# A decoder trunk's MLP: chunks with on-chip operands, against two phases with DRAM operands and a one-level Strassen product

## The chip, the core and the metric

The kernel runs on one core of a Trainium2 chip as a single launch. The metric is the device time of that launch in microseconds (us), lower is better. The profile is one further execution of the same program, taken by the hardware profiler. TensorE does the matmuls (PE in the profile, PEld for its weight loads), VectorE is DVE, ScalarE is ACT, GpSimd is POOL, and SyncE (SP) issues most of the DMAs.

## The reference, cut to what matters

A trunk of two layers on 1024 tokens of width 1024. Each layer has an attention mixer (compressed, selected and window attention in layer 0, sliding-window attention with sinks in layer 1) and an MLP, with norms and gates around both. The change is in the MLP:

```python
def squared_relu_mlp(h, w_up, w_down):      # h (1024, 1024), w_up (1024, 4096), w_down (4096, 1024)
    a = jax.nn.relu(h @ w_up)
    return (a * a) @ w_down

for i in range(DEPTH):                      # DEPTH = 2
    ...
    h = modulate(rms_norm(x, norm_g[i, 2]), sh2, sc2)
    y = squared_relu_mlp(h, mlp_w_up[i], mlp_w_down[i])
    x = x + (1 + g2)[:, None, :] * rms_norm(y, norm_g[i, 3])
```

All values are float32.

## The kernel before

Every large product is made of float32 operands split exactly into a high and a low float32r part. `mm3` (lines 558 to 563) adds hi*hi, hi*lo and lo*hi into one PSUM bank, so one product of a 128-row contraction tile costs three matmuls of 128x128 by 128x512, each with its own weight load. `weight` (line 539) loads a 512 KB piece of a weight matrix into one of three `raw` buffers, ACT copies it to the high part `wh` (line 554), and DVE subtracts to get the low part `wl` (line 555). Both parts take one 4 KB-per-partition buffer each from the pool of 37 slots, from which nearly all large tiles come. Small tiles of 2 KB per partition come from the tag `t2` with 8 buffers. PSUM has eight banks, handed out in turn by `bank`.

The MLP walks over the 4096 hidden features in tiles of 128, in chunks of two tiles (14 chunks, then one of four; `CHUNKS`). In a chunk, `up` computes the hidden tile for both halves of the tokens (eight contraction tiles, 24 matmuls for each half). ACT takes relu out of PSUM and squares it into the high part `ah`, DVE squares it again (line 1226) and subtracts to get the low part `al` (line 1227). Then `down` multiplies: for each of eight token tiles t and two column halves h, the chunk's two hidden tiles (6 matmuls) are summed in a PSUM bank, and `evac` adds the bank to the running sum `y[t]` in SBUF (line 1242; chunk 0 copies on ACT instead). Left operands never leave SBUF. The next chunk's weights are loaded among these steps.

The program is emitted as a list of main steps of about 1.3 us of TensorE each (`go`), with other steps spread among them (`spread`), or queued to run some steps later (`later`, `chain`). The scheduler of the tile framework then fixes an order for each engine, and buffers are handed out as they come free. In layer 0 the 56 `side` steps, each a 512 KB load of `ada_w` (into the same three `raw` buffers) and a DVE multiply-add (line 315), are spread over all chunks of the MLP.

When the last chunk has finished token tile t, `post` runs: it loads the residual `x`, squares and sums y on ACT (line 502), multiplies by the gate row (line 503; on POOL for the first seven tiles of layer 1, otherwise on DVE), takes the root on POOL (line 440), adds into x on DVE (line 511) and stores x. In layer 0 `finish_tile` then norms the tile (line 461), and after each fourth tile turns four of them into h^T, with a split on DVE (lines 487 and 488). Layer 1's first projection follows at once. In layer 1 the launch ends there.

Of the kernel before, what the change touches and what calls it, by code (L numbers as in the profile page):

```python
# [9 lines left out]
F32 = mybir.dt.float32  # L10
# [19 lines left out]
NCH = [2] * 14 + [4]  # L30
CHUNKS = [range(sum(NCH[:c]), sum(NCH[:c + 1])) for c in range(len(NCH))]
# [47 lines left out]
def spread(a, b):  # L79
    """The steps of b with those of a evenly among them, each before a step of b."""  # L80
    out, n = [], 0
    for k, f in enumerate(b):
        while n < len(a) and n * len(b) <= k * len(a):
            out.append(a[n])
            n += 1
        out.append(f)
    return out + a[n:]


class Trunk:  # L90
    """Products in float32: every operand is split exactly into hi + lo (both float32r), and
    hi*hi + hi*lo + lo*hi accumulate in PSUM."""
# [228 lines left out]
    def ada_cols(self, l, m, acc, dst):  # L321
        """dst [128, 8]: the chunk's values, feature k*128+p at [p, k]."""
# [18 lines left out]
    def ada_first(self):  # L341
        """As ada_pre for the first norm, by halves of the features: half(h) gives the loads and the steps."""
# [52 lines left out]
    def ada_pre(self, l, which, raw=None):  # L395
        """Steps of A = g (1 + scale) and B = shift as columns, for the norm before mixer (0) or MLP (1)."""
# [13 lines left out]
    def ada_gate(self, l, which):  # L410
        """Steps of (1 + gate) g of the norm after mixer (0) or MLP (1), a row in DRAM."""
# [37 lines left out]
    def norm_stages(self, x, out, t):  # L449
        """out[t] = x / rms(x)"""  # L450
# [41 lines left out]
    def gated(self, y, x, gate, eng=None):  # L492
        """(steps for the halves of y, stages after them) of x += gate * y / rms(y); y(h): [128, 512]."""
# [21 lines left out]
    def finish_tile(self, t, x, xr, col, hT):  # L515
        """Norms a finished token tile; after the fourth of a half also turns them into h^T."""
# [41 lines left out]
    def mm3(self, out, s, m, first, last):  # L558
        """out += s.T @ m with s, m = (hi, lo)."""
# [5 lines left out]
    def weights(self, w, rows, c0, n, eng=None, turned=False):  # L565
        """(steps, list): the steps fill the list with (hi, lo) [128, n] for each of the row tiles of w."""
# [8 lines left out]
    def product(self, out, terms, evac):  # L575
        """Main steps: out() = the sum of s.T @ m over terms (functions that give s, m), then evac."""
# [67 lines left out]
    def rope(self, t, src, dst, nh):  # L644
        """dst (SBUF [128, nh*64]) = rotated src (PSUM)."""
# [28 lines left out]
    def vstack(self, src, dst):  # L674
        """dst [128, n, 128] = (hi | lo) of src [128, n * 64] in PSUM."""
# [5 lines left out]
    def nsa_project(self, hT, w):  # L681
        """Chunks (loads, main steps) of the projections and of the compression."""
# [4 lines left out]
        # kc, vc: X[z][r // 6][64 * (r % 2):][:, r % 6 // 2, i, head] is hi (z = 0) or lo (1) of token 16 i + r;  # L687
        # at i = 64 + y it is pe[16 y + r]
# [102 lines left out]
    def compress(self, X, m):  # L791
        """(loads, main steps) of the compressed keys (m = 0) or values (1)."""
# [61 lines left out]
    def q_load(self, i, j, two):  # L854
        """[128 (hi, lo: d), 4 heads, 128 tokens]; loaded together with that of the next block (two = 0) or group (1)"""
# [17 lines left out]
    def masked(self, out, s, mask, nm, init):  # L873
        """out = -(s + mask) / 8 and nm = its minimum (the maximum's negative)."""
# [45 lines left out]
    def o_out(self, o, o32):  # L920
        """o32 [128, 2, 128] = the two halves of o's partitions added, heads on their partitions."""
# [69 lines left out]
    def kv_load(self, j):  # L991
        """Steps that load the K^T stacks (selected, window) and the V stacks (selected, window) of kv head j."""
# [14 lines left out]
    def nsa_unit(self, i, j):  # L1007
        """Steps of the scores and of the products with V for block i, kv head j."""
# [5 lines left out]
        def scale(ps, l, b):  # L1014
            """scales the four P by gate / l"""
# [104 lines left out]
    def importance(self, pc):  # L1120
        """The blocks' importance [128, 16] from the four heads' probabilities."""
# [10 lines left out]
    def select(self, i, imp):  # L1132
        """The mask (0 or NEG) of the selected blocks and of the causal bound, [128, (i + 1) * 128]."""
# [407 lines left out]
```

## Time and profile before

| | |
|---|---|
| Time, median of 3 runs (lowest to highest) | 2641.11 us (2639.13 to 2643.16) |
| Span of the profiled execution, first to last instruction | 2637.3 us |
| Median of the runs less that span | 3.8 us |
| Mean granted TensorE clock | 0.988 |
| PE busy | 2543.5 us, 96% of the span |
| DVE, ACT, POOL busy | 1691.7, 1098.3 and 648.6 us |
| Moved by DMA | 271.37 MB, 103 GB/s over the span |

A matmul's busy time overlaps that of the next one, so PE's rate is read from the starts of matmuls or from their number in a stretch, not from their durations. A granted clock of 1.00 is the higher of TensorE's two levels, 2.4 GHz.

### The profile page before, as it was taken

The numbers are of one execution on the slowest core, as the hardware profiler recorded it, in microseconds if no ns is written. First come the engines' busy times: TensorE is split into PE (matmuls) and PEld (weight loads), VectorE is DVE, ScalarE is ACT, GpSimd is POOL, SyncE is SP. The second block draws the span as 40 slices with busy tenths as digits, with TensorE's granted clock in tenths as the row PEclk, the third lists the DMA queues.
The fourth block names the chain that finished last, engine by engine and source line by source line (L and its number), as shares of the span: only waits on it lengthen the run. The fifth ranks groups of instructions, "written<-read, shape, count | busy, mean of one in ns | idle before, by whom it ended". The sixth has DMA issues, their size and how long they took to land.

```text
span 2637.3 us, 35655 instructions
## 1 busy us (share of the span) xinstructions
PE 2543.5 (96%) x12742; PEld 2125.0 (81%) x12742; DVE 1691.7 (64%) x3739; ACT 1098.3 (42%) x2451; POOL 648.6 (25%) x904
## 2 busy tenths in 40 slices
PE   6999999999989999999999999889999999999998
PEld 4789888888877788888888888767788888888887
DVE  6875589999975756565656477577744544444445
ACT  3642478898862421212121244477742121212122
POOL 4431666556641000000000004487600000000003
PEclk8999999999999999999999999989999999999999
DMA  7388412212256533233323244353221111111113
GB/s 269 119 286 254 156 65 82 79 50 77 65 125 149 158 96 96 80 112 97 95 80 96 64 147 154 107 153 87 65 72 56 42 57 46 56 40 56 40 49 135
DMA packets 199656, 271.37 MB, mean 103 GB/s; under 512 B 12388, under 2 KB 136504, under 8 KB 199480
## 3 DMA queue, kind: packets, MB, share of 16 engines
q1 hardware_dynamic: 170680, 239.74, 28.9%
q0 software_dynamic: 28800, 29.36, 4.6%
q8 instruction: 100, 1.64, 0.3%
q14 instruction: 76, 0.62, 0.1%
HBM read 213.47 MB, written 55.59 MB: 102 GB/s over the span
## 4 chain that ended last, share of the span: by engine, by line
PE 56%; DVE 5%; POOL 2%; issue 2%; ACT 1%; DMA 1%; POOLq 0%; DVEq 0%; ACTq 0%
PE b L561 18%; PE b L563 18%; PE b L562 18%; DVE p L875 1%; DVE x L511 1%; POOL r L440 1%; DVE wl L555 0%; DMA adaw<-in_ada_w_dram 0%; PE b L871 0%; POOL qv L626 0%; POOL p L1332 0%; DVE yg L503 0%; DVE pT L901 0%; DVE hl L488 0%; PE o L916 0%
## 5 line engine op out<-in xcount | busy, mean ns | idle before, releaser
L561 PE MATMUL b<-hh,wh 128*128 128x512 f32 x1344 | 524.9, 392 | 3.9 <-DVE hh L487 2.0
L562 PE MATMUL b<-hl,wh 128*128 128x512 f32 x1344 | 525.5, 391 | 0.3 <-DVE hl L488 0.2
L563 PE MATMUL b<-hh,wl 128*128 128x512 f32 x1344 | 524.2, 390 | 1.2 <-DVE wl L555 1.2
L1242 DVE TENSOR_TENSOR y<-b,y 128x512 f32<-128x512 f32 x448 | 306.3, 689 | 190.0 <-PE b L563 188.8
L561 PE MATMUL b<-wh,ah 128*128 128x512 f32 x1024 | 399.7, 390 | 0.0
L562 PE MATMUL b<-wl,ah 128*128 128x512 f32 x1024 | 398.4, 389 | 0.0
L563 PE MATMUL b<-wh,al 128*128 128x512 f32 x1024 | 397.5, 389 | 0.0
L554 ACT ACTIVATE wh<-w 128x1024 fp32r<-128x1024 f32 (+1 forms) x183 | 212.2, 1162 | 367.9 <-PE b L562 299.3
L1224 ACT ACTIVATE r<-b 128x512 f32<-128x512 f32 x128 | 76.1, 595 | 628.9 <-PE b L563 628.9
L555 DVE TENSOR_TENSOR wl<-w,wh 128x1024 fp32r<-128x1024 f32 (+1 forms) x171 | 229.1, 1341 | 155.7 <-ACT wh L554 87.2
L561 PEld LDWEIGHTS b<-hh,wh 128*128 128x128 f32 x1344 | 252.9, 188 | 57.5 <-ACT wh L554 2.3
L563 PEld LDWEIGHTS b<-hh,wl 128*128 128x128 f32 x1344 | 253.0, 188 | 54.1 <-DVE wl L555 1.9
L562 PEld LDWEIGHTS b<-hl,wh 128*128 128x128 f32 x1344 | 253.1, 188 | 52.9 <-DVE hl L488 1.6
L879 ACT ACTIVATE p<-p,nm 128x256 f32<-128x256 f32 (+7 forms) x384 | 250.4, 656 | 55.3 <-DVE nm L875 52.6
L440 POOL TENSOR_TENSOR r<-ms,mhalf 128x1 f32<-128x1 f32 x64 | 46.0, 725 | 853.8 <-DVE ms L439 848.5
L1226 DVE TENSOR_TENSOR r<-r 128x512 f32<-128x512 f32 x128 | 88.4, 691 | 247.1 <-ACT ah L1225 246.6
L1019 POOL TENSOR_SCALAR p<-p,rl,gate 128x640 f32<-128x640 f32 (+7 forms) x256 | 199.4, 791 | 134.4 <-DVE rl L1017 83.1
L901 DVE TENSOR_TENSOR pT<-b,pT 128x512 fp32r<-128x512 f32 (+1 forms) x334 | 214.8, 656 | 17.5 <-ACT pT L900 15.8
L563 PEld LDWEIGHTS b<-wh,al 128*128 128x128 f32 x1024 | 192.2, 188 | 39.9
L561 PEld LDWEIGHTS b<-wh,ah 128*128 128x128 f32 x1024 | 192.2, 188 | 39.7
L562 PEld LDWEIGHTS b<-wl,ah 128*128 128x128 f32 x1024 | 192.3, 188 | 39.6
L900 ACT ACTIVATE pT<-b 128x512 fp32r<-128x512 f32 (+1 forms) x334 | 185.6, 578 | 42.6 <-PE b L894 33.9
(241 smaller groups left out, 4294.7 us busy)
## 6 DMA issues: line engine op xcount, KB each, us to landing
adaw<-in_ada_w_dram SPq DMA_DIRECT2D x96, 512.0 KB, 4.2
w<-in_mlp_w_up_dram SPq DMA_DIRECT2D x64, 512.0 KB, 4.2
w<-in_mlp_w_down_dram SPq DMA_DIRECT2D x64, 512.0 KB, 3.6
x<-x SPq DMA_DIRECT2D x48, 512.0 KB, 3.4
w<-in_nsa_w_in_dram SPq DMA_DIRECT2D x18, 512.0 KB, 5.9
x<-in_x_dram SPq DMA_DIRECT2D x16, 512.0 KB, 5.6
kv<-k POOLq DMA_DIRECT2D x16, 512.0 KB, 4.9
qd<-qh SPq DMA_DIRECT2D x32, 256.0 KB, 2.1
```

Of the source, the lines that this page charges most:

```text
L554: nc.scalar.activation(h_, r_, AF.Copy)
L555: (eng or (nc.gpsimd if early else nc.vector)).tensor_tensor(l_, r_, h_.bitcast(F32), op=ALU.subtract)
L561: mm(out, s[0], m[0], start=first, stop=False)
L562: mm(out, s[0], m[1], start=False, stop=False)
L563: mm(out, s[1], m[0], start=False, stop=last)
L879: self.nc.scalar.activation(p, p, AF.Exp, scale=-1.0, bias=nm, accum_out=l)
L900: nc.scalar.activation(x[:, 0, 0:w], pt[:, 0:w], AF.Copy)
L901: nc.vector.tensor_tensor(x[:, 1, 0:w], pt[:, 0:w], x[:, 0, 0:w].bitcast(F32), op=ALU.subtract)
L1019: nc.gpsimd.tensor_scalar(ps[g], ps[g], rl[:, g:g + 1], gate[:, g, b:b + 1], op0=ALU.mult, op1=ALU.mult)
L1224: nc.scalar.activation(r, pt, AF.Relu)
L1226: nc.vector.tensor_tensor(r, r, r, op=ALU.mult)
L1242: nc.vector.tensor_tensor(y[t][:, sl], pt, y[t][:, sl], op=ALU.add)
```

## The change

The MLP becomes two phases. `mlp_up` computes all 32 hidden tiles of the layer one after another. For each it keeps a float32 tile u (relu on ACT, one square on DVE, no split). For every pair q of hidden tiles (a, b) `combine` makes five sums or differences of token halves on POOL, and SP writes seven left operands of 128x512 to a DRAM tile: b1, a0+b1, b0-b1, a0+b0, a1-a0, a0 and a1+b1, where a0 is the first half of the tokens of tile a.

`mlp_down` computes the second product as a one-level Strassen product: contraction halves are the even and the odd hidden tiles, row halves the token halves, column halves those of the output. It makes four passes g over the 16 pairs q. Passes 0 to 2 compute two of the seven products each, pass 3 the seventh. A product has four token tiles, one PSUM bank each, and is summed over the whole contraction in that bank. So passes 0 to 2 hold all eight banks for 16 items (g, q), and pass 3 four. For each item `load` brings the left operands and W_down rows from DRAM (1.25 MB in passes 0 and 2, 1.0 in pass 1, 0.5 in pass 3, in units of 1024 x 1024 bytes); `prep` makes the right operand's sums on POOL (two adds, one, two, none) and splits both operands (high part on ACT, low part on DVE). Loads are emitted three items ahead, the splits one item ahead. At the end of a pass `evac` adds and subtracts the banks into y. Token tiles 0 to 3 are finished by pass 2 and go to `post` during pass 3; tiles 4 to 7 finish one after another in the last four items, which run token tile by token tile.

The 56 side steps of layer 0 are now spread over `mlp_up` alone. Comments and docstrings are removed, which changes no instruction. The core of the diff:

```diff
-NCH = [2] * 14 + [4]
-CHUNKS = [range(sum(NCH[:c]), sum(NCH[:c + 1])) for c in range(len(NCH))]
+UT = HID // P
...
-        def down(Wd, A, t, h, c):
...
+    def mlp(self, hT, w_up, w_down, first, side, post, last):
+        sd = self.mlp_up(hT, w_up, first, side)
+        self.mlp_down(sd, w_down, post, last)
+
+    def mlp_up(self, hT, w_up, first, side):
...
+        def up(u, hf):
+            def evac(pt):
+                if hf == 0:
+                    U[u] = self.slot("u", F32, [P, 2, 512])
+                r = self.t2("r")
+                nc.scalar.activation(r, pt, AF.Relu)
+                nc.vector.tensor_tensor(U[u][:, hf], r, r, op=ALU.mult)
+                if hf == 1 and u % 2 == 1:
+                    self.later(lambda: self.chain(combine(u // 2)), 1)
...
+        def combine(q):
+            a, b = U.pop(2 * q), U.pop(2 * q + 1)
+            d = self.tc.dram_tile([P, 7, 512], F32, name=f"s{self.n}_{q}")
...
+            def put():
+                nc.sync.dma_start(d[:, 0], b[:, 1])
+                nc.sync.dma_start(d[:, 5], a[:, 0])
+                nc.sync.dma_start(d[:, 1:3], z[0])
+
+            def put2():
+                nc.sync.dma_start(d[:, 3:5], z[1])
+                v = self.t2("sy")
+                nc.gpsimd.tensor_tensor(v, a[:, 1], b[:, 1], op=ALU.add)
+                nc.sync.dma_start(d[:, 6], v)
+
+            A, B = ALU.add, ALU.subtract
+            return [two(0, (a[:, 0], b[:, 1], A), (b[:, 0], b[:, 1], B)), put,
+                    two(1, (a[:, 0], b[:, 0], A), (a[:, 1], a[:, 0], B)), put2]
+
+        order = [(0, 0), (1, 0), (0, 1), (1, 1)] + [(u, hf) for u in range(2, UT) for hf in range(2)]
...
+        self.go(spread(side, steps))
...
+    def mlp_down(self, sd, w_down, post, last):
...
+        items = [(g, q) for g in range(4) for q in range(n_q)]
...
+        def load(g, q):
+            m = 1 if g == 3 else 2
+            s, w = (self.slot(x, F32, [P, 2, 512]) for x in ("sr", "wr"))
+            nc.sync.dma_start(s[:, 0:m], sd[q][:, 2 * g:2 * g + m])
...
+                nc.sync.dma_start(w, two(rows[g < 2]))
+                e = None
+                if g != 1:
+                    e = self.t2("we")
+                    nc.sync.dma_start(e, rows[0][:, 0:512] if g == 0 else rows[1][:, 512:1024])
...
+            def sums():
...
+                if g == 0:
+                    t(w[:, 0], w[:, 0], e, op=ALU.subtract)
+                    t(w[:, 1], w[:, 1], e, op=ALU.add)
+                elif g == 1:
+                    t(w[:, 0], w[:, 0], w[:, 1], op=ALU.add)
+                elif g == 2:
+                    t(w[:, 0], w[:, 0], w[:, 1], op=ALU.add)
+                    t(w[:, 1], w[:, 1], e, op=ALU.subtract)
+
+            def split(k):
...
+                nc.scalar.activation(hi, r, AF.Copy)
+                nc.vector.tensor_tensor(lo, r, hi.bitcast(F32), op=ALU.subtract)
+                ready.setdefault((g, q), []).append((hi, lo))
...
+        def evac(g, z, b):
+            o, c = banks.pop((z, b)), b + 4
+            if (g, z) == (0, 0):
+                copy(b, 0, o), copy(c, 0, o)
+            elif (g, z) == (0, 1):
+                add(b, 0, o), copy(c, 1, o)
+            elif (g, z) == (1, 0):
+                add(b, 0, o)
+            elif (g, z) == (1, 1):
+                copy(b, 1, o), add(b, 0, o, ALU.subtract)
+            elif (g, z) == (2, 0):
+                add(c, 1, o)
+            elif (g, z) == (2, 1):
+                add(b, 1, o), add(c, 1, o)
+                self.later(lambda: post(b, y[b]), 12 * b + 4)
+            else:
+                add(c, 0, o), add(c, 1, o, ALU.subtract)
+                self.later(lambda: post(c, y[c]), 0)
+
+        def mms(g, q, z, b):
+            if q == 0:
+                banks[z, b] = self.bank()
+            s, t = (tuple(v[:, z] for v in x) for x in ready[g, q])
+            self.mm3(banks[z, b], tuple(v[:, b * P:b * P + P] for v in s), t, q == 0, q == n_q - 1)
+            if q == n_q - 1:
+                evac(g, z, b)
+
+        TAIL = 4
+        main = [[lambda z=z, b=b, g=g, q=q: (mms(g, q, z, b), mms(g, q, z, b + 1)) for z in range(2 - (g == 3)) for b in (0, 2)]
+                for g, q in items[:-TAIL]]
+        tail = items[-TAIL:]
+        main.append([lambda b=b, k=k: [mms(*tail[j], 0, b) for j in (k, k + 1)] for b in range(4) for k in range(0, TAIL, 2)])
...
+        for n, steps in enumerate(main):
+            extra = [f for k in ahead(n + 1) for f in prep(*items[k])]
+            upto = min(len(items), n + 4 + max(0, n - len(main) + 2 * TAIL))
+            extra = [lambda k=k: load(*items[k]) for k in range(loaded, upto)] + extra
...
+            self.go(spread(extra, steps))
```

## Rows read from the trace of the kernel before

**Rows 1.** The page's line of busy time by engine.

```profile
PE 2543.5 (96%) x12742; PEld 2125.0 (81%) x12742; DVE 1691.7 (64%) x3739; ACT 1098.3 (42%) x2451; POOL 648.6 (25%) x904
```

**Rows 2.** Stretches: length, engines' busy time (instructions), clock, DMA share, GB/s.

```profile
132.00:198.00 66.00, 60.77 (x380) 54.90 (x381) 51.44 (x69) 27.53 (x33) 20.82 (x12) 0.95 0.86 287
881.00:1589.00 708.00, 704.93 (x3183) 581.18 (x3183) 420.31 (x571) 180.65 (x265) 8.08 (x12) 1.00 0.33 102
1740.00:1752.00 12.00, 4.64 (x17) 3.24 (x18) 12.00 (x31) 11.38 (x28) 11.85 (x14) 0.63 0.65 209
1929.00:2630.00 701.00, 700.58 (x3107) 579.93 (x3105) 337.75 (x458) 160.09 (x248) 22.91 (x23) 1.00 0.19 57
2050.00:2500.00 450.00, 450.00 (x1987) 372.59 (x1987) 219.27 (x292) 84.87 (x120) 0.00 (x0) 1.00 0.16 47
```

**Rows 3.** Timeline of PE in layer 1's MLP: start, duration, instruction.

```profile
2100.38 0.39 PE L561 MATMUL b<-wh,ah 128*128 128x512 f32 x1
...
2101.06 0.39 PE L561 MATMUL b<-wh,ah 128*128 128x512 f32 x1
```

**Rows 4.** By line, 2050 to 2500: count, busy us, mean ns, idle.

```profile
L1242 DVE TENSOR_TENSOR y<-b,y 128x512 f32<-128x512 f32 x171 | 118.2, 691 | 91.2 <-PE b L563 90.5
...
L555 DVE TENSOR_TENSOR wl<-w,wh 128x1024 fp32r<-128x1024 f32 x41 | 50.1, 1222 | 42.6 <-PE b L562 42.6
L554 ACT ACTIVATE wh<-w 128x1024 fp32r<-128x1024 f32 x40 | 42.0, 1049 | 0.0
...
L1227 DVE TENSOR_TENSOR al<-r,ah 128x512 fp32r<-128x512 f32 x40 | 27.6, 690 | 1.0
...
L1224 ACT ACTIVATE r<-b 128x512 f32<-128x512 f32 x40 | 24.0, 599 | 349.7 <-PE b L563 349.7
```

**Rows 5.** By line, whole run, same columns.

```profile
L315 DVE SCALAR_TENSOR_TENSOR ada<-adaw,cond,ada 128x1024 f32<-128x1024 f32 x70 | 90.0, 1286 | 65.5 <-DMA adaw<-in_ada_w_dram 65.2
...
L511 DVE SCALAR_TENSOR_TENSOR x<-yg,r,x 128x1024 f32<-128x1024 f32 x32 | 41.6, 1301 | 14.8 <-POOL r L440 14.7
...
L487 DVE CAST hh<-h 128x512 fp32r<-128x512 f32 x64 | 28.1, 467 | 15.4 <-ACT h L485 12.5 <-PE b L871 2.9
...
L461 DVE TENSOR_SCALAR xr<-x,r 128x1024 f32<-128x1024 f32 x32 | 24.6, 780 | 17.8 <-POOL r L440 17.0 <-PE b L562 0.7
...
L503 POOL TENSOR_TENSOR yg<-y,gbc 128x512 f32<-128x512 f32 x14 | 18.0, 1294 | 665.0 <-DVE y L1242 665.0
```

**Rows 6.** Timeline of DVE in layer 0's projections.

```profile
141.28 1.22 DVE L555 TENSOR_TENSOR wl<-w,wh 128x1024 fp32r<-128x1024 f32 x1
142.97 1.77 DVE L555 TENSOR_TENSOR wl<-w,wh 128x1024 fp32r<-128x1024 f32 x1 [0.47 <-ACT wh L554]
145.22 1.75 DVE L555 TENSOR_TENSOR wl<-w,wh 128x1024 fp32r<-128x1024 f32 x1 [0.48 <-ACT wh L554]
```

**Rows 7.** Timeline of POOL in the same stretch.

```profile
143.62 2.27 POOL L626 TENSOR_TENSOR qv<-qv,qr 128x512 f32<-128x512 f32 x1
146.64 1.48 POOL L628 TENSOR_TENSOR qr<-qv,qh 128x512 f32<-128x512 f32 x1 [0.75 <-ACT qh L627]
```

**Rows 8.** DMA issues, whole run: count, KB each, us to landing.

```profile
w<-in_mlp_w_up_dram SPq DMA_DIRECT2D x64, 512.0 KB, 4.2
w<-in_mlp_w_down_dram SPq DMA_DIRECT2D x64, 512.0 KB, 3.6
...
qd<-qr SPq DMA_DIRECT2D x32, 256.0 KB, 2.0
```

**Rows 9.** Waits in layer 0's MLP, 960 to 1500: total us, times, longest.

```profile
ACT wh L554 <- PE b L562: 266.5, 29, 19.3
...
DVE ada L315 <- DMA adaw<-in_ada_w_dram: 37.8, 20, 5.0
```

**Rows 10.** Timeline of DVE at the end of the run.

```profile
2629.71 0.68 DVE L1242 TENSOR_TENSOR y<-b,y 128x512 f32<-128x512 f32 x1
...
2632.26 1.28 DVE L511 SCALAR_TENSOR_TENSOR x<-yg,r,x 128x1024 f32<-128x1024 f32 x1 [0.66 <-POOL r L440]
```

More of the change, by code (lines that the diff above doesn't have):

```diff
@@ L1231, in up @@
             return self.product(self.bank, [lambda k=k: term(k) for k in range(KT)], evac)
-        def down(Wd, A, t, h, c):
-            sl = slice(h * 512, h * 512 + 512)
-            def evac(pt):
-                if c == 0:
-                    if h == 0:
-                        y[t] = self.slot(name="y")
-                    nc.scalar.activation(y[t][:, sl], pt, AF.Copy)
-                else:
-                    nc.vector.tensor_tensor(y[t][:, sl], pt, y[t][:, sl], op=ALU.add)
-                if c == nch - 1 and h == 1:
-                    post(t, y[t])
-            def term(u):
-                return tuple(v[:, t * P:(t + 1) * P] for v in A[u]), tuple(v[:, sl] for v in Wd[u])
-            return self.product(self.bank, [lambda u=u: term(u) for u in range(len(CHUNKS[c]))], evac)
@@ L1250, in mlp, with two, f @@
-        side = list(side)
-        for c in range(nch):
-            (_, W), (dload, Wd) = loads
-            A, ups, downs = [], [], []
-            for hf in range(2):
-                for u in range(len(CHUNKS[c])):
-                    if hf == 0:
-                        ups.append(lambda: A.append((self.slot("ah", F32R), self.slot("al", F32R))))
-                    ups += up(W, A, u, hf)
-            for t in range(NT):
-                for h in range(2):
-                    downs += down(Wd, A, t, h, c)
-            nxt = last
-            if c + 1 < nch:
-                loads = self.mlp_loads(w_up, w_down, c + 1)
-                nxt = loads[0][0]
-            k = -(-len(side) // (nch - c))
-            n = 0 if c + 1 < nch else len(ups) // 2
-            self.go(spread(side[:k], ups[:n] + spread(dload, ups[n:]) + spread(nxt, downs)))
-            side = side[k:]
+        def combine(q):
+            a, b = U.pop(2 * q), U.pop(2 * q + 1)
+            d = self.tc.dram_tile([P, 7, 512], F32, name=f"s{self.n}_{q}")
+            sd.append(d)
+            z = {}
+            def two(n, *ops):
+                def f():
+                    z[n] = self.slot("sx", F32, [P, 2, 512])
+                    for k, (x, y, op) in enumerate(ops):
+                        nc.gpsimd.tensor_tensor(z[n][:, k], x, y, op=op)
+                return f
+            def put():
[10 more added lines that the diff above has]
+                    two(1, (a[:, 0], b[:, 0], A), (a[:, 1], a[:, 0], B)), put2]
@@ new lines, in mlp_up, with prep, new, copy @@
+        order = [(0, 0), (1, 0), (0, 1), (1, 1)] + [(u, hf) for u in range(2, UT) for hf in range(2)]
+        steps = []
+        for n, (u, hf) in enumerate(order):
+            ld = [loads[u + 2 - (n < 4) * u + (n < 4) * (n - 2)]] if (n >= 4 and hf == 0 and u + 2 < UT) or n in (2, 3) else []
+            steps += spread(ld, up(u, hf))
+        self.go(spread(side, steps))
+        return sd
+    def mlp_down(self, sd, w_down, post, last):
+        nc = self.nc
+        n_q = len(sd)
+        items = [(g, q) for g in range(4) for q in range(n_q)]
+        y, raw, ready, banks = [None] * NT, {}, {}, {}
+        def load(g, q):
+            m = 1 if g == 3 else 2
+            s, w = (self.slot(x, F32, [P, 2, 512]) for x in ("sr", "wr"))
+            nc.sync.dma_start(s[:, 0:m], sd[q][:, 2 * g:2 * g + m])
+            rows = [w_down[(2 * q + x) * P:(2 * q + x + 1) * P] for x in range(2)]
+            two = lambda r: r.rearrange("p (h c) -> p h c", h=2)
+            if g == 3:
+                nc.sync.dma_start(w[:, 0], rows[0][:, 0:512])
+                e = None
+            else:
+                nc.sync.dma_start(w, two(rows[g < 2]))
+                e = None
+                if g != 1:
+                    e = self.t2("we")
+                    nc.sync.dma_start(e, rows[0][:, 0:512] if g == 0 else rows[1][:, 512:1024])
+            raw[g, q] = s, w, e
+        def prep(g, q):
+            u = {}
+            def sums():
+                s, w, e = u["r"] = raw.pop((g, q))
+                t = nc.gpsimd.tensor_tensor
+                if g == 0:
[7 more added lines that the diff above has]
+            def split(k):
+                r = u["r"][k]
+                if g == 3:
+                    h = self.slot("st", F32R, [P, 2, 512])
+                    hi, lo, r = h[:, 0:1], h[:, 1:2], r[:, 0:1]
+                else:
+                    hi, lo = (self.slot("st", F32R, [P, 2, 512]) for _ in range(2))
+                nc.scalar.activation(hi, r, AF.Copy)
+                nc.vector.tensor_tensor(lo, r, hi.bitcast(F32), op=ALU.subtract)
+                ready.setdefault((g, q), []).append((hi, lo))
+            return [sums, lambda: split(0), lambda: split(1)]
+        def new(t, h):
+            if y[t] is None:
+                y[t] = self.slot(name="y")
+            return y[t][:, h * 512:h * 512 + 512]
+        def copy(t, h, o, eng=None):
+            if eng:
+                eng.tensor_copy(new(t, h), o)
+            else:
+                nc.scalar.activation(new(t, h), o, AF.Copy)
+        def add(t, h, o, op=ALU.add):
+            v = y[t][:, h * 512:h * 512 + 512]
+            nc.vector.tensor_tensor(v, v, o, op=op) if op == ALU.subtract else nc.vector.tensor_tensor(v, o, v, op=op)
+        def evac(g, z, b):
[13 more added lines that the diff above has]
+                self.later(lambda: post(b, y[b]), 12 * b + 4)
+            else:
+                add(c, 0, o), add(c, 1, o, ALU.subtract)
[12 more added lines that the diff above has]
+        main.append([lambda b=b, k=k: [mms(*tail[j], 0, b) for j in (k, k + 1)] for b in range(4) for k in range(0, TAIL, 2)])
+        ahead = lambda n: [n] if n < len(items) - TAIL else list(range(len(items) - TAIL, len(items))) if n == len(items) - TAIL else []
+        loaded = 3
+        for n in range(loaded):
+            load(*items[n])
+        for f in prep(*items[0]):
+            f()
+        for n, steps in enumerate(main):
+            extra = [f for k in ahead(n + 1) for f in prep(*items[k])]
+            upto = min(len(items), n + 4 + max(0, n - len(main) + 2 * TAIL))
+            extra = [lambda k=k: load(*items[k]) for k in range(loaded, upto)] + extra
+            loaded = upto
+            if len(main) - n <= 8:
+                extra += last[:-(-len(last) // (len(main) - n))]
+                last = last[-(-len(last) // (len(main) - n)):]
+            self.go(spread(extra, steps))
@@ L1456, in run @@
                     else:
-                        steps = spread(first[0][0], steps)
+                        steps = spread(first[0][:2], steps)
                     self.go(steps)
@@ L1478, in run @@
                 out(NT - 1)
-                self.go(spread(first[0][0], extra))
+                self.go(spread(first[0][:2], extra))
             self.mark("mlp")
```

24 lines of the change are left out of this document (6 added, 18 removed).

## The prediction

> **What bounds the kernel now.** Read the busy line first: PE is busy 96% of the span, and DVE, next, 64% [rows 1]. A share over a span hides stages, so the stretches come next. The MLP of layer 1 fills 1929 to 2630, that of layer 0 roughly 881 to 1589; inside layer 1's, from 2050 to 2500, PE is busy for all of 450.0 us at clock 1.00 while DVE works 219.3, ACT 84.9, POOL 0, and DMA engines are at a share of 0.16 [rows 2]. The reader is to see one saturated engine and four with room. PE's rate comes from its starts: one trio takes 2101.06 - 2100.38 = 0.68 us, 0.2267 us a matmul [rows 3], and the count agrees, 450/1987 = 0.2265 [rows 2]. One MLP has 2 x 1536 = 3072 matmuls, 696.4 us at that rate. The stretches of the two layers are 708 and 701 [rows 2], so some 12 and 5 us of the two MLPs are anything else. There is little to win here but matmuls.
>
> **Removed.** For each pair of hidden tiles `down` now makes 8 x 2 x 2 = 32 three-matmul sums; the new phase makes 7 x 4 = 28. That is 12 matmuls less for each of 16 pairs in two layers, 384, at 0.2267: 87.0 us, all on PE. DVE also loses the accumulation (691 ns, 448 times in all) and the low part of the hidden tile (690 ns), ACT one square; they had slack, so this counts for nothing by itself [rows 4].
>
> **The first phase.** PE's 1536 matmuls are unchanged, 348.2 us. For each pair (21.8 us) POOL gets five 128x512 adds of 1.29 [rows 5], 6.5 us, on an engine that is idle here. SP gets five stores of 1.84 MB together (29.4 MB a layer). In layer 0 the 56 loads of `ada_w` (29.4 MB) now fall into this half, beside W_up's 16.8 MB: 75.5 MB in 348 us, 217 GB/s. The nearest row is 132 to 198, 287 GB/s at share 0.86, which is 333 at a full share [rows 2]; so 0.65. A W_up piece holds a `raw` buffer for 4.2 (landing) + 1.05 + 1.22 = 6.5 us [rows 4, 8], an `ada_w` piece for about 4.2 + 1.29 = 5.5 [rows 5]: 32 x 6.5 + 56 x 5.5 = 516 us of holding in 348, half of what three buffers offer (1044). Bounds: nothing, or, if two of the three buffers were lost to waiting in turn, 516 - 348 = 168. DVE did wait for `ada_w` 20 times, 37.8 us, in 540 us of the old kernel, and PE did not feel it [rows 2, 9]. I take 2 us.
>
> **The second phase, in its steady state.** An item of passes 0 to 2 is 24 matmuls, 5.44 us of PE. Against it:
> - ACT: two copies of 1024 at 1.05 = 2.1 us [rows 4].
> - DVE: two subtractions of 1024 at 1.22 = 2.4 us [rows 4].
> - POOL: at most two adds at 1.29 = 2.6 us [rows 5].
> - DMA: 1.31 MB (passes 0 and 2), 241 GB/s; over a layer 64 x 1.05 = 67.1 MB in 1344 x 0.2267 = 304.7 us, 220 GB/s, a share of 0.66 by the same 333.
>
> Each alone has half of the time free, so the loads and splits, emitted one to three items ahead, are hidden by PE. But DVE and POOL are not independent. Where both ran two-input operations, DVE's subtractions ended at 144.74 and 146.97 and took 1.77 and 1.75 instead of 1.22, and POOL's ended at 145.89 and 148.12 after 2.27 and 1.48 [rows 6, 7]. One of each ends every 2.23 us. So an item's two pairs need 4.46 us of the 5.44: covered, with 18% to spare, and I add nothing. The Trainium skill (SBUF — State Buffer, "Who interferes with whom") says that a DVE instruction with two SBUF inputs and a GpSimd instruction that reads SBUF exclude each other for the whole instruction. By that the two pairs would need 2 x (1.22 + 1.29) = 5.02 us, still under 5.44; the rows give 4.46, so they overlap somewhat more than that rule allows.
>
> **Ends of passes.** All eight banks close within one item. After pass 0, twelve ACT copies of 0.60 and four DVE adds of 0.69; after pass 1, four copies and eight adds; after pass 2, twelve adds [rows 4]. A bank is wanted again one item after its last matmul, 4.1 to 5.4 us later, by the first use in the next pass. ACT's 7.2 us run beside the 5.44 us of the closing item and are wanted one by one, so they just fit if no split stands before them. Bounds: none, or all of the longer engine's work in the open, 7.2 + 5.5 + 8.3 = 21 us a layer, 42 in all. The copies are wanted in the order in which they come, so I take 3.
>
> **Other seams.** Between phases, item 0 needs only its loads and splits, ready long before: 1 us a layer; at worst a load, an add pair and a split in the open, 3.6 + 2.6 + 1.05 + 1.22 = 8.5 each [rows 4, 5, 8]. In layer 0's pass 3 (192 matmuls, 43.5 us) DVE has 16 x 2 x 0.69 = 22.1 of splits, 8.3 of closing pass 2, four token tiles' `post` and norm at 2 x 0.69 + 1.30 + 0.78 = 3.5 (13.8), eight h^T splits at 0.47 + 0.69 (9.3) and four weight splits (4.9): 58.4 us [rows 4, 5]. That is 15 over, unless splits were made ahead while pass 2 left DVE idle. Bounds 0 and 15; I take 5. The last four token tiles then need 2.72 us of PE each but 3.5 + 1.4 of DVE, so layer 1 begins with a backlog of 9 us and the 9.3 of h^T behind it; the first projection has 16 x 6 x 0.2267 = 21.8 us of work on the first token half as cover: 3 us, bounds 0 and 10. At the very end two adds instead of one follow the last matmul, and `post` comes every 2.72 us instead of 5.44; the end chain from the add to the last DVE write was 2633.54 - 2629.71 = 3.8 us [rows 10] and grows by 2; bounds 0.7 (the extra add) and 4.6 (that, and one token tile's 2 x 1.29 on POOL and 1.30 on DVE in turn).
>
> **The sum.** -87.0 + 2 + 3 + 2 + 5 + 3 + 2 = -70.0. Against the profiled execution: 2637.3 - 70.0 = 2567.3, and with the 3.8 us around its span 2571.1; the median of the runs shown, 2641.1, stands for the same. I forecast 2571 us, with 2554 (every seam free) to 2588 for this case.
>
> **The rivals.**
> 1. *Passes close in the open.* Speaks for it: eight banks are all that there are, and none is left to rotate into. Against: the next pass wants them in the order of their closing. Time: 42 in place of 3, 2571 + 39 = 2610. The Trainium skill (Perfetto Trace Analysis, "Matmuls" under Optimizing Tensor Performance) asks that groups rotate through banks so that emptying one overlaps the next group; here that overlap exists only across passes. Chance 0.10.
> 2. *DVE and POOL become the bound of passes 0 and 2.* For: rows 6 show DVE idle another 0.47 before each contended subtraction, waiting for ACT. If that stays, an item is 2 x (1.22 + 1.29 + 0.48) = 5.98 us, 0.54 more than PE, in 64 items: +35, 2606. Against: splits of later items are independent, so the wait should be filled. It binds from 5.44 us an item on. Chance 0.08.
> 3. *Layer 0 is crowded:* the first phase's buffers or pass 3's DVE cost their 15 to 25 more: 2586 to 2596. For: ACT stood up to 19.3 us before a buffer that PE had to free [rows 9], so work ahead is limited by the 37 slots. Chance 0.10.
> 4. *The loads don't keep up: slower.* If the stream has one transfer in flight, an item takes 3.6 + 3.6 + 2.0 = 9.2 us in passes 0 and 2, 7.2 in pass 1 and 4.0 in pass 3 [rows 8]: 16 x (18.4 + 7.2 + 4.0) = 474 a layer against 304.7, +338 in all, 2571 + 338 = 2909. It decides below 67.1 MB in the old 348 us, 193 GB/s. And a PE that waits pays more: in 1740 to 1752 it was busy for 4.64 of 12 us and was granted 0.63 of the clock [rows 2]. Against: 287 GB/s in 132 to 198, with several transfers under way. Chance 0.08; a rate just at that threshold, no change within 0.2% (5 us, about what a measurement of this kernel can tell from no change), 0.03.
>
> My forecast keeps 0.61. Faster is 0.61 + 0.10 + 0.08 + 0.10 = 0.89, the same 0.03, slower 0.08. The range 2554 to 2612 takes in the forecast and the first three rivals.
>
> **What the profile would show.** Right: PE's count down by 384 512-column matmuls at 0.2267 us, both second phases some 305 to 315 us long with PE without gaps, DMA near 220 GB/s there, DVE and POOL under their item time. Wrong: PE waiting for `st` tiles (DVE or ACT: rival 2 or 3), for banks at three places a layer (rival 1), or DVE and POOL waiting for `sr`, `wr` or `we` from DMA all through the phase (rival 4). The sign turns if PE loses 87.0/128 = 0.68 us in each item of the two layers.

## The result, and the profile after

The changed kernel takes 2612.7 us (median; 2610.0 to 2613.3) against 2641.4: a ratio of 0.989, interval 0.9876 to 0.9904. It is faster by 28.7 us, where 70 were forecast, and lies 0.7 us above the forecast's range. The sign and the mechanism were right; more than half of the gain went somewhere. The busy line of the page, to set beside [rows 1]:

```profile
PE 2470.1 (95%) x12358; PEld 2062.8 (79%) x12358; DVE 1698.8 (65%) x3419; ACT 1186.6 (45%) x2515; POOL 1201.1 (46%) x1224
```

PE has 384 instructions less, as counted. The span is 2608.3 against 2637.3 us. PE's busy time fell by 73.4 us instead of 87.0, and its idle time rose by 44.4. So the matmuls are gone, and 13.6 + 44.4 = 58 us of something else have come where the forecast had 17, some 41 more. Seven stretches (columns as in [rows 2]) cut the two MLPs at their phases:

```profile
886.00:1250.00 364.00, 354.87 (x1603) 290.99 (x1601) 199.55 (x206) 73.96 (x106) 123.92 (x77) 0.99 0.60 200
1250.00:1264.00 14.00, 0.57 (x2) 0.49 (x2) 2.42 (x3) 3.25 (x4) 8.70 (x7) 0.62 0.90 327
1264.00:1587.00 323.00, 320.30 (x1416) 265.10 (x1416) 230.67 (x214) 148.04 (x191) 146.87 (x88) 0.99 0.67 227
1926.00:2275.00 349.00, 346.11 (x1543) 286.69 (x1541) 115.69 (x112) 72.79 (x104) 129.00 (x76) 1.00 0.40 134
2275.00:2285.00 10.00, 0.79 (x2) 0.70 (x3) 3.67 (x3) 2.99 (x4) 9.05 (x7) 0.62 0.56 194
2285.00:2595.00 310.00, 307.30 (x1344) 253.88 (x1342) 207.92 (x172) 127.51 (x166) 161.08 (x96) 0.99 0.67 224
2595.00:2608.00 13.00, 0.37 (x2) 0.00 (x0) 7.90 (x15) 2.89 (x8) 4.08 (x6) 0.63 0.53 193
```

The reader is to see two stretches in which PE does next to nothing, the 14 and 10 us between the phases. Layer 1's second phase is some 6 us over its 304.7 us of matmuls. Layer 0's first phase is 15 longer than layer 1's, for 60 short instructions more. From the start of PE's last matmul to the span's end it is 13.3 us (2608.3 - 2594.98), where it was 8.1 (2637.3 - 2629.20).

**Between the phases.** What ended the waits, 1249 to 1264 and then 2274 to 2285 (total, times, longest):

```profile
POOL sx L1243 <- DVE u L1225: 19.9, 1, 19.9
...
PE b L560 <- ACT st L1315: 13.4, 1, 13.4
...
ACT row L426 <- PE b L424: 9.0, 1, 9.0
...
POOL sx L1243 <- DVE u L1225: 15.0, 1, 15.0
...
PE b L560 <- ACT st L1315: 9.7, 1, 9.7
ACT st L1315 <- POOL wr L1301: 7.0, 1, 7.0
```

PE waits for the split of item 0's `wr` in both layers, but not for the same reason. (These waits count from the modelled end of a matmul; from the start of the last one to the start of the next it is 13.8 and 10.1 us.) The timeline of SP in layer 0:

```profile
1231.75 0.32 SPq L1255 DMA_DIRECT2D s<-sy  x1
1249.72 0.28 SPq L427 DMA_DIRECT2D gate<-row  x1
1250.06 1.29 SPq L1289 DMA_DIRECT2D we<-in_mlp_w_down_dram  x3
1251.44 0.38 SPq L1278 DMA_DIRECT2D sr<-s  x1
```

For 18 us SP issues nothing. Its next entry stores a gate row that ACT can write only after PE's transposition, at the very end of the phase, and item 0's loads stand behind it. In layer 1 there is no such store, and the loads go out from 2261.41. There the timeline of POOL and ACT shows the other reason:

```profile
2275.95 1.26 POOL L1243 TENSOR_TENSOR sx<-u,u 128x512 f32<-128x512 f32 x1 [14.99 <-DVE u L1225]
...
2277.16 2.24 POOL L1243 TENSOR_TENSOR sx<-u 128x512 f32<-128x512 f32 x1
2279.37 1.25 POOL L1254 TENSOR_TENSOR sy<-u,u 128x512 f32<-128x512 f32 x1
...
2280.59 1.25 POOL L1300 TENSOR_TENSOR wr<-wr,we 128x512 f32<-128x512 f32 x1
...
2281.81 1.25 POOL L1301 TENSOR_TENSOR wr<-wr,we 128x512 f32<-128x512 f32 x1
...
2283.10 1.06 ACT L1315 ACTIVATE st<-wr 128x1024 fp32r<-128x1024 f32 x1 [7.01 <-POOL wr L1301]
```

POOL stands 15.0 us at the sums of the last pair, which need the square of PE's last product. Item 0's sums come after three of that pair's operations.

**The steady state** is as forecast. DVE's splits and POOL's sums in pass 0 of layer 1:

```profile
2299.12 2.19 DVE L1316 TENSOR_TENSOR st<-wr,st 128x1024 fp32r<-128x1024 f32 x1
2300.18 2.27 POOL L1301 TENSOR_TENSOR wr<-wr,we 128x512 f32<-128x512 f32 x1
2301.23 2.31 DVE L1316 TENSOR_TENSOR st<-sr,st 128x1024 fp32r<-128x1024 f32 x1
2302.41 2.28 POOL L1300 TENSOR_TENSOR wr<-wr,we 128x512 f32<-128x512 f32 x1
...
2303.58 2.19 DVE L1316 TENSOR_TENSOR st<-wr,st 128x1024 fp32r<-128x1024 f32 x1
```

DVE's splits end at 2301.31, 2303.54 and 2305.77, one every 2.23 us, and an item's two pairs take 4.46 of its 5.44 us. That it is the very number that was read from [rows 6, 7] is in part luck: there an operation of 1.75 us and an idle 0.48 made up the 2.23, here there is no idle time between the splits. From 2286 to 2372 PE is busy for all of 86.00 us. The Trainium skill (SBUF — State Buffer, "Who interferes with whom") would have the two exclude each other, 1.22 + 1.29 = 2.51 us a pair; the 2.23 measured is under that here too. Most of that difference comes of adding durations, which hold a tail that the next operation overlaps: alone, DVE's splits start every 1.14 us (1356.61, 1357.75, 1358.89) and POOL's sums every 1.22 (2279.37, 2280.59, 2281.81), 2.36 together.

**The end of pass 0** is the third place. ACT in layer 0:

```profile
1347.78 4.03 ACT L1330 ACTIVATE y<-b 128x512 f32<-128x512 f32 x8 [15.72 <-PE b L562]
...
1351.61 1.13 ACT L1315 ACTIVATE st<-sr 128x1024 fp32r<-128x1024 f32 x1
...
1352.56 1.65 ACT L1330 ACTIVATE y<-b 128x512 f32<-128x512 f32 x3
...
1353.99 1.16 ACT L1315 ACTIVATE st<-wr 128x1024 fp32r<-128x1024 f32 x1
...
1355.20 1.58 PE L560 MATMUL b<-st,st 128*128 128x512 f32 x4 [2.70 <-ACT st L1315]
```

The split of item (1,0) stands among the copies that close pass 0. ACT stood 15.7 us at the first of these copies, until PE had finished that bank, with the split behind it; POOL's sums for the split had been done by 1335.4. PE goes on at 1355.20 after 2.7 us idle (3.1 from start to start), and likewise at 2375.84. PE's waits name no other stop in either second phase.

**The fourth place** is in layer 0's first phase, where PE folds each `ada` column (L337):

```profile
1239.85 0.60 ACT L1224 ACTIVATE r<-b 128x512 f32<-128x512 f32 x1 [4.84 <-PE b L562]
1240.48 0.69 DVE L1225 TENSOR_TENSOR u<-r 128x512 f32<-128x512 f32 x1 [3.53 <-ACT r L1224]
1241.09 1.27 DVE L333 TENSOR_REDUCE adas<-adat 128x16 f32<-128x512 f32 x2
...
1242.42 0.25 PE L337 MATMUL b<-adas,fold 128*32 128x8 f32 x8 [2.60 <-DVE adas L333]
```

DVE had nothing to do from 1236.95 on, but the reductions stand behind a square that waits for PE's product in hand, and the fold stands right behind that product. PE's waits in that phase (886 to 1250) begin with:

```profile
PE b L337 <- DVE adas L333: 5.7, 3, 2.7
PE b L560 <- DVE hh L486: 2.5, 1, 2.5
```

PE lost 5.7 us at three of the seven folds (2.7, 2.6 and 0.4), and was granted 0.50 of the clock behind the two longer ones (936.0 to 939.3, 1243.3 to 1246.5). Before the change PE's waits in layer 0's whole MLP (885 to 1592) name no fold:

```profile
PE b L561 <- DVE hh L487: 2.0, 2, 1.2
PE b L425 <- DVE adag L421: 0.8, 2, 0.4
PE b L562 <- DVE hl L488: 0.2, 1, 0.2
```

The same two lists show **a fifth place**, the start of the first phase, where PE takes up the second half of h^T (`hh`): 2.5 us in layer 0, with the clock at 0.51 right after it (898.4 to 901.8), and 2.4 in layer 1, against 2.0 in all before. With the slow stretch that is some 4.5 us more. No run took it alone.

### The profile page after: what moved, and what is told of

The parts are those of the page before. It is cut to its first block, busy times and chain, and to the rows that moved or that the text cites. A ratio compares the mean times of both kernels' runs of the same rounds, so it can differ in the third digit from the quotient of the medians.

```text
span 2608.3 us, 36408 instructions
## 1 busy us (share of the span) xinstructions
PE 2470.1 (95%) x12358; PEld 2062.8 (79%) x12358; DVE 1698.8 (65%) x3419; ACT 1186.6 (45%) x2515; POOL 1201.1 (46%) x1224
## 4 chain that ended last, share of the span: by engine, by line
PE 75%; DVE 10%; issue 4%; DMA 4%; POOL 3%; ACT 2%; SPq 1%; POOLq 0%; DVEq 0%; ACTq 0%
PE b L560 20%; PE b L562 20%; PE b L561 20%; PE b L870 4%; PE o L915 4%; PE b L893 4%; DVE p L874 2%; DMA o<-o 1%; DVE pT L900 1%; DMA adaw<-in_ada_w_dram 1%; PE b L1023 1%; POOL qv L625 1%; PE b L476 1%; DVE wl L554 1%; DVE x L510 1%
## 5 line engine op out<-in xcount | busy, mean ns | idle before, releaser
L560 PE MATMUL b<-st,st 128*128 128x512 f32 x896 | 337.9, 398 | 28.6 <-ACT st L1315 28.6
L561 PE MATMUL b<-st,st 128*128 128x512 f32 x896 | 349.6, 390 | 0.0
L562 PE MATMUL b<-st,st 128*128 128x512 f32 x896 | 349.2, 390 | 0.0
L1243 POOL TENSOR_TENSOR sx<-u,u 128x512 f32<-128x512 f32 x64 | 96.6, 1510 | 455.4 <-issue 319.1
L1225 DVE TENSOR_TENSOR u<-r 128x512 f32<-128x512 f32 x128 | 94.4, 739 | 314.5 <-ACT r L1224 314.4
L1316 DVE TENSOR_TENSOR st<-sr,st 128x1024 fp32r<-128x1024 f32 (+1 forms) x128 | 193.0, 1507 | 122.6 <-ACT st L1315 121.6
L560 PEld LDWEIGHTS b<-st,st 128*128 128x128 f32 x896 | 171.3, 192 | 65.8 <-ACT st L1315 30.3
L1315 ACT ACTIVATE st<-sr 128x1024 fp32r<-128x1024 f32 (+1 forms) x128 | 122.5, 957 | 212.1 <-PE b L561 164.6
L554 DVE TENSOR_TENSOR wl<-w,wh 128x1024 fp32r<-128x1024 f32 (+2 forms) x107 | 193.7, 1811 | 37.3 <-ACT wh L553 32.5
L893 PE MATMUL b<-ident,p 128*128 128x128 f32 x1296 | 192.5, 273 | 5.7 <-DVE nm L874 4.1
L561 PEld LDWEIGHTS b<-st,st 128*128 128x128 f32 x896 | 169.1, 189 | 35.2
```

The costliest lines, as they stand in the source:

```text
L554: (eng or (nc.gpsimd if early else nc.vector)).tensor_tensor(l_, r_, h_.bitcast(F32), op=ALU.subtract)
L560: mm(out, s[0], m[0], start=first, stop=False)
L561: mm(out, s[0], m[1], start=False, stop=False)
L562: mm(out, s[1], m[0], start=False, stop=last)
L893: nc.tensor.transpose(pt[:, g * P:(g + 1) * P], p[:, cols], self.ident)
L1315: nc.scalar.activation(hi, r, AF.Copy)
```

## The experiments

The theory: the forecast's mechanism holds, and the missing 41 us lie in seams (places where one stretch of work hands over to the next) at which an in-order queue holds work that is ready. The rival: the buffers and engines are full, so that a seam mended here opens there.

**1. Item 0 prepared inside the first phase** (prep_early).

```diff
+        N = len(steps)
+        steps.insert(N - 8, lambda: load(0, 2))
+        steps.insert(N - 12, lambda: [f() for f in prep(0, 0)])
+        steps.insert(N - 16, lambda: load(0, 1))
+        steps.insert(N - 24, lambda: load(0, 0))
         self.go(spread(side, steps))
...
-        for n in range(loaded):
-            load(*items[n])
-        for f in prep(*items[0]):
-            f()
```

> Item 0 of the second phase is loaded, summed and split inside the last 24 steps of the first phase, in both layers; all else stays. Theory (the hand-over is what was mis-sized: PE stands 13.8 us in layer 0 and 10.1 us in layer 1 because item 0's operands come late, and its first matmuls then run at half the clock, about 1.7 us each): both gaps under 1 us, the low clock after them gone, 2612.7 - 13.8 - 10.1 - 3.4 = 2585 us (2582 to 2591). Rival (the buffers are all in use, so earlier work on item 0 only moves the wait into the first phase): 2605 or more, with new PE gaps before the last relu.

2586.2 us (ratio 0.9793, 0.978 to 0.9806), 26.5 under the changed kernel. PE has no wait from 2255 to 2270, and from 1240 to 1260 only a fold's 2.6. The theory holds for this seam.

**2. Only SP's order in layer 0** (gate_on_act).

```diff
-                nc.sync.dma_start(d.rearrange("o (k p) -> (o k) p", p=P), row)
+                (nc.scalar if (l, which) == (1, 1) else nc.sync).dma_start(d.rearrange("o (k p) -> (o k) p", p=P), row)
```

> The store of layer 1's second gate row (L427), behind which item 0's loads stand on SP in layer 0, goes out from ACT's queue instead; POOL's order stays. Theory (SP's queue makes the loads late in layer 0, and POOL's order is the next wait): the loads of layer 0 go out some 10 us earlier; the last pair's three operations end at 1255.3 as before, the sums at 1257.8, the copy at 1258.9, so layer 0's gap falls from 13.8 to about 9.3 us; layer 1's stays at 10.1; 2612.7 - 4.5 = 2608 (2606 to 2610). Rival (SP's queue is not what holds the loads): they still go out at 1250, 2612.

2607.5 us (0.9872, 0.9859 to 0.9886). The loads now go out some 18 us earlier against the phase's end:

```profile
1229.32 3.94 SPq L1289 DMA_DIRECT2D we<-in_mlp_w_down_dram  x3
1233.35 0.38 SPq L1278 DMA_DIRECT2D sr<-s  x1
...
1248.94 1.26 POOL L1243 TENSOR_TENSOR sx<-u,u 128x512 f32<-128x512 f32 x1 [20.06 <-DVE u L1225]
```

PE's wait falls only from 13.4 to 10.0, since POOL's order is the next thing late, as in layer 1. In layer 0 two queues held the same work, one behind the other.

**3. Only POOL's order** (combine_late, combine_late_2).

```diff
-                    self.later(lambda: self.chain(combine(u // 2)), 1)
+                    self.later(lambda: self.chain(combine(u // 2)), 1 + LATE * (u == UT - 1))
```

with LATE = 8; combine_late_2 has besides `n_q = UT // 2` and the last pair's `sy` on DVE.

> Only the combine of the last pair of hidden tiles is emitted 8 steps later, so that POOL comes to item 0's sums before it waits for the last square; the loads stay where they are. Theory (two causes: in layer 1 POOL's queue stands 15.0 us at the last pair with the loads already landed, in layer 0 the loads themselves go out only at 1250 us): layer 1's gap falls from 10.1 to 1 to 2 us, layer 0's stays at 12 to 14; 2612.7 - 9 - 1.5 = 2602 (2599 to 2606). Rival (POOL's order sets both): both gaps under 3 us, 2588. Rival (the loads set both): nothing moves, 2612.

2569.3 us (0.9725, 0.9711 to 0.9738), but it leaves out the last pair in both second phases: `n_q` is read off a list that had 15 entries then. Its 168 matmuls less (12190) are 38.1 us, so it stands for 2607.4. PE's longest wait for `st` at the hand-over falls to 6.2 us in one layer and 6.3 in the other. In layer 1 `sy` still stood ahead of item 0's sums; in layer 0 the new order had also put the loads of `sr` and `wr` ahead of the gate row. Neither theory had that, so this run alone tells little.

> As combine_late, with all 16 pairs in the second phase again and the last pair's one remaining operation (its sum `sy`) on DVE, so that nothing of the last pair stands on POOL ahead of item 0's sums in either layer; in layer 0 the loads of `we` still stand on SP behind the gate row's store. Theory (POOL's queue held layer 1, SP's queue holds layer 0): layer 1's gap 10.1 to at most 2 us; layer 0's stays at the 6.6 us that combine_late showed, with the sums starting when `we` lands; 2612.7 - 8.5 - 1.7 - 7.2 - 1 = 2594 (2590 to 2598). Rival (the loads of item 0 come too late in layer 1 as well): layer 1's gap stays at 5 us or more, 2600.

2600.2 us (0.9845, 0.9832 to 0.9859), between the two. PE's waits, layer 0 (1249 to 1280) and layer 1 (2270 to 2300):

```profile
PE b L561 <- ACT st L1316: 6.5, 1, 6.5
PE b L562 <- DVE st L1317: 0.8, 1, 0.8
...
PE b L561 <- ACT st L1316: 3.4, 2, 2.4
PE b L562 <- DVE st L1317: 2.0, 2, 1.3
```

Layer 1's first wait is 2.4 instead of 9.7: POOL's order was most of it. What is left is the loads: POOL's first sum starts at 2270.61, and the first `we`, issued at 2262.21 behind six other loads, took 8.2 us to land (the profile names a matmul as POOL's releaser, but 2262.21 + 8.2 is 2270.4). Layer 0's 6.5 is `we` behind the gate row, as said. The rival had a part: the loads are not early in layer 1 either, only less late than POOL.

**4. The end of pass 0, from both sides** (copies_on_dve; split_ahead, which stands with the mends below).

```diff
+        DV = nc.vector
...
-                copy(b, 0, o), copy(c, 0, o)
+                copy(b, 0, o), copy(c, 0, o, DV)
```

> Four of the twelve PSUM copies that close pass 0 go to DVE instead of ACT. Theory (pass 0 closes partly in the open: the split of item (1,0) stands on ACT behind copies that wait for their banks, PE stands 3.1 us in each layer and then runs 3.4 us at half the clock): ACT comes to the split 2.4 us earlier; gaps 3.1 to under 1 us in both layers, 2612.7 - 2 x 2.3 - 2 x 1.7 = 2605 (2602 to 2609). Rival (DVE with eight operations of 0.69 us takes ACT's place): gaps still about 3 us, 2612.

2607.2 us (0.9869, 0.9856 to 0.9883), 5.5 under the changed kernel. In each layer PE's 2.7 us become three short waits of 1.0, 0.6 and 0.3, and no slow stretch follows. The wait of 1.0 is for a copy on ACT, so for a bank, once the split no longer comes last; this run therefore says less on splits against banks than split_ahead does.

**5. The folds** (fold_later, fold_later_2): L337 in `ada_cols` becomes a function of its own.

```diff
-        pt = self.bank()
-        for z in range(4):
-            nc.tensor.matmul(pt[32 * z:32 * z + 32, 0:8], self.fold, part[:, z::4], start=True, stop=True)
+        def fold():
+            pt = self.bank()
+            for z in range(4):
+                nc.tensor.matmul(pt[32 * z:32 * z + 32, 0:8], self.fold, part[:, z::4], start=True, stop=True)
...
+        self.later(fold, FOLD)
```

with FOLD = 3. The DVE add behind the fold, what uses its column, and the gate row's transposition and store move with it.

> In layer 0's first phase PE's fold of each `ada` column (L337) is emitted three main steps after the two reductions that it reads. Theory (PE, in order, waits 3.13 and 2.99 us at folds whose reductions stand on DVE behind a square that waits for PE's own next product, and runs 3.4 us at half the clock after each): those gaps go, 2612.7 - 5.6 - 1.0 - 3.4 = 2603 (2600 to 2606). Rival (DVE is simply full there, and the wait comes back elsewhere): 2610 to 2613.

2579.0 us (0.9768, 0.9755 to 0.9781), with the last pair left out in layer 0 (84 matmuls, 19.0 us): the list of delayed work is served in order, and the last combine came behind a fold.

> As fold_later, with all 16 pairs in layer 0's second phase (fold_later had left out the last pair there, 84 matmuls, 19.0 us). Theory: layer 0's first phase 9 us shorter, as in fold_later's trace, and the hand-over of layer 0 shorter because the last pair's combine now comes behind a fold and so behind item 0's sums; 2579.0 + 19.0 = 2598 us (2594 to 2603). Rival (the full phase takes the gain back): 2606 or more.

2595.6 us (0.9825, 0.9812 to 0.9839), 17.1 under the changed kernel. Layer 0's first phase, from its first relu to its last, takes 353 us instead of 364:

```profile
887.00:1240.00 353.00, 349.62 (x1602) 287.53 (x1601) 203.41 (x204) 74.70 (x107) 128.13 (x77) 1.00 0.66 218
```

So 11 us went there, 9 to 10 of them the folds': the slow stretch at the phase's start is absent in this run too (898 to 902 at clock 1.00), and no cause is shown for that. The other 6 or so of the 17.1 go with the hand-over, which this order shortens too: PE's wait there is 5.3 us instead of 13.4. The row speaks against full buffers: the same work, with a greater DMA rate, fits into less time.

**6. The end of the run** (tail_of_8): `TAIL = 4 if last else 8`.

> In layer 1 the last 8 items, not 4, are taken token tile by token tile, so that `post` of the last tiles comes every 5.44 us of PE instead of 2.72. Theory (the end of the run is set by a backlog of DVE and POOL after the last matmul, 9.2 us to DVE's last write against some 4.3 before the change): the backlog falls by 3 to 4 us, 2609 (2608 to 2610). Rival (one tile's own chain is what remains): no change, 2612 to 2613.

2616.9 us (0.9909, 0.9896 to 0.9923), 4.1 slower. The end shrinks by 1.6 us (from the start of the last matmul, at 2603.27, 11.7 us), but eight items need their splits at once, and without the hand-over PE now waits 5.3 us for `st` in that phase instead of 2.7. There is a backlog, and this is no way to be rid of it.

**7. The mends together.**

> Item 0 prepared inside the first phase (as prep_early), four copies of pass 0 on DVE, the folds three steps later, and the last 8 items by token tile in layer 1, all together. Theory (what was missing against the forecast lies in these seams, and the steady state is as forecast): from prep_early's 2586.2, less 5.5, less three folds of 2.8 and three slow stretches of 1.7 each, less 3: 2564 us (2558 to 2572), about the forecast of 2571. Rival (the seams pass their waits on to each other, as one buffer pool serves them all): 2578 or more.

2582.8 us (0.9783, 0.977 to 0.9796): against 2564, the rival's side, and the longer tail is in it.

> prep_early, copies_on_dve and fold_later_2 together, with the end of layer 1 as it was (4 items by token tile). Theory (the gains add, since each is a place of its own; four_mends lost by its longer tail, whose first items PE waited for): 2586.2 - 5.5 - 9 = 2572 (2567 to 2577), the time that was forecast. Rival (the seams share one pool of buffers and pass their waits on): 2580 or more.

2578.7 us (0.9764, 0.9751 to 0.9778), between the two. One part of the difference can be seen at the end of pass 0 in layer 1, three_mends first, then prep_early, which has no mend there:

```profile
2345.80:2349.20 3.40, 3.40 (x9) 2.60 (x8) 3.40 (x3) 3.40 (x5) 1.43 (x1) 0.51 0.05 19
```

```profile
2353.60:2357.00 3.40, 3.35 (x15) 2.77 (x16) 3.16 (x3) 3.40 (x5) 0.00 (x0) 1.00 0.59 169
```

After waits of 1.3, 0.6 and 0.4 us PE ran at half the clock in the one, after a single wait of 2.7 at full clock in the other. The copies on DVE, worth 5.5 us alone, were worth nothing in layer 1 here. Another part stands in layer 0's first phase: at 1093.6 PE waits 3.4 us for DVE's `adag` column (L433), and the clock is 0.57 right after it, 1093.6 to 1097. That is some 4 us more than in prep_early and in fold_later_2, which show a wait of 0.8 there; why the column comes later with the mends together is open. New waits did appear, as the rival has it, but no buffer is seen to pass them on.

In split_ahead the split is moved in place of the copies:

```diff
-                extra = [f for k in ahead(n + 1) for f in prep(*items[k])]
+                extra = [f for k in (ahead(n + 1) + [n + 2] * (n + 2 == UT // 2)) * (n + 1 != UT // 2) for f in prep(*items[k])]
```

> As three_mends, but with the closing of pass 0 mended at the other end: all twelve copies stay on ACT, and item (1,0) is summed and split one item earlier, so that its split of `sr` and `wr` stands on ACT ahead of the copies that wait for banks. Theory (PE waits there for a split that stands behind copies, not for the copies or the banks themselves): gap 3.09 to under 0.5 us in both layers and no slow clock after it, 2586.2 - 9.2 - 9 = 2568 (2563 to 2573). Rival (banks: the next pass waits for the copies themselves): a gap of 2 us or more stays, 2577.

2573.8 us (0.9744, 0.9731 to 0.9757). That is 0.8 above the theory's range, but its waits are as it said: all twelve copies are on ACT, in the same banks, and PE's waits in layer 1's second phase (2252 to 2558) are an empty list. The stretch:

```profile
2253.00:2558.00 305.00, 304.94 (x1345) 251.92 (x1343) 209.03 (x172) 129.41 (x167) 160.40 (x96) 1.00 0.69 233
```

1344 matmuls at the 0.2267 of [rows 3] are 304.7 us. In layer 0 ACT stands before the same copies:

```profile
1329.72 4.03 ACT L1345 ACTIVATE y<-b 128x512 f32<-128x512 f32 x8 [12.47 <-PE b L571]
```

but the split of item (1,0)'s `wr` had started at 1316.18, ahead of them, and PE is busy for all of 1334 to 1341 at clock 1.00. So it was the place of a split in ACT's queue, not the eight banks. The stop of 3.4 us at the `adag` column is in this run too (1096.4).

> As split_ahead, with token tile 6's product by the gate row at the end on DVE (2 x 0.68 us) instead of POOL (2 x 1.27). Theory (after the last matmul tile 7's root of the mean square stands on POOL behind those two products): the end comes 1 to 2 us earlier, 1 to 2 us under split_ahead. Rival (DVE's own queue sets the end): 1 us later.

It is split_ahead with `PT = 6` for 7. 2572.5 us (0.9738, 0.9724 to 0.9751), 1.3 less than split_ahead, whose interval overlaps. From the start of the last matmul to the end its profile shows 13.8 us against 13.3: the rival's direction, by half of its 1 us, so the theory does not hold, and what else differs lies elsewhere. What would shorten the end stays open. Both versions beat both kernels, by 68.3 and 69.6 us against the one before.

## Why the prediction was off

**The step that failed** is "Between phases, item 0 needs only its loads and splits, ready long before: 1 us a layer". The two hand-overs measured 13.8 and 10.1 us, and the first matmuls after each ran at the lower clock, some 27 us in all where 2 were forecast; with item 0 early, 26.5 us went (experiment 1). Two things were wrong in it. Nothing in the code makes item 0 early: its loads are emitted behind the first phase's last steps, and SP and POOL, in order, kept them or their sums behind entries that wait for PE's last product. And the upper bound of 8.5 left out that the last pair's three POOL operations come first. This is some 25 of the 41 us.

**Terms mis-sized.** Ends of passes: 3 forecast; 2 x (2.7 + 1.7) = 9 by the waits and the slow stretches, all of it at pass 0; split_ahead took it away. The working had named the condition, "if no split stands before them"; what cost was a split behind the copies. First phase: 2 forecast, for loads; the loads kept up (200 GB/s, where 217 was worked out), but the folds, at which PE had not waited before, cost some 9 by their waits and slow stretches (fold_later's first phase is 355 us instead of 364), and the h^T starts some 4.5. End of the run: 2 forecast with a bound of 4.6, 5.2 measured. Two terms were too large: in layer 0's pass 3, 5 forecast, PE is busy for all of 1525 to 1587 at clock 1.00, so nothing; at the start of layer 1, 3 forecast, some 1 by PE's waits. Against the forecast that is +25 (hand-over), +6, +12, +3, -5 and -2, together 39 of the 41 us; the rest is not placed.

**Right:** the 384 matmuls and their 0.2267; PE without gaps in both second phases but for pass 0's end, and DMA at 224 to 227 GB/s there; 4.46 us of DVE and POOL an item. With three seams mended the time is 2573.8, 2.8 off the forecast. That closeness is partly luck: hand-over, pass ends and folds then cost little against the 7 us that the forecast had for them, and pass 3 nothing against 5, while the end, the h^T starts and the stop at the `adag` column cost what it had not.

**The rivals.** 1 (passes close in the open) came in part, 9 of 42 us, and not through banks. 2 did not occur: POOL is busy 73.94 of 86 us in layer 1's pass 0, and PE does not feel it; its 5.98 us an item had counted the idle 0.48 besides the work, where the 2.23 of [rows 6] already held it. 3 (layer 0 is crowded) has a part of its size, some 9 us instead of 15 to 25, but neither of its two causes: the folds cost it, not buffers or pass 3's DVE. 4 did not occur. The rival that was missing is the hand-over itself: the working never followed SP's and POOL's queues across it.

## What to carry to other kernels

Where one phase's last work and the next phase's first share an in-order queue, write out that queue across the seam on each engine, SP too: whatever stands ahead and waits for the bound engine's last result puts the next phase's start behind it, however early its data could be there. Price a seam by that list, not by the work that the first item needs. And when work that was thinly spread is pressed into half of its time, look for the small steps in which the bound engine reads another's result, and give those a step's distance.

## What the runs showed of the hardware

A PE that had stood for some microseconds mostly came back at the lower of its two levels. After the 2.7 us at pass 0's end, and between the phases, both in layer 0:

```profile
1355.80:1359.20 3.40, 3.40 (x10) 2.64 (x9) 3.19 (x4) 3.40 (x5) 0.37 (x1) 0.50 0.41 141
...
1253.40:1267.10 13.70, 3.58 (x9) 2.83 (x10) 4.79 (x4) 4.27 (x5) 9.99 (x7) 0.50 1.00 377
```

0.50 of the clock is 1.2 GHz. In either row PE is busy for some 3.5 us of it, half of which is lost, so each such stop cost about 1.7 us more than it lasted. But a stop of the same 2.7 us in prep_early was followed by full clock (the rows in experiment 7). Of the 16 such stops at pass 0's end in the eight runs that leave it as it is, 14 were followed by the lower level and two by full clock, so a stop's length alone does not say which. The second row also has DMA at a full share with 377 GB/s, where 333 had been worked out from [rows 2]; in combine_late_2, 2262 to 2272, it was 396 at 1.02. At such a rate a single load of 256 KB (`we`) took 8.2 us from its issue to its landing, against a median of 3.4 over all of `after`: a burst of loads at a seam is fast as a whole and late for the one that is wanted first.
